# Inverse variance applied to the residual blocks after their last accumulation instead of to the last super-round's activations

## Chip, cores and metric

The kernel runs on one core of one Trainium2 chip. The metric is the device time of one execution in microseconds (us). Before the change three timed runs gave 1086.19, 1089.17 and 1089.94 us; the median is 1089.17 us. The profile that is read below is that of a further execution, which took 1083.84 us. The engines are named as in the profile: PE is TensorE (PEld its weight loads), DVE is VectorE, ACT is ScalarE, POOL is GpSimd and SP is SyncE.

## What is computed

Two layers of a transformer-like trunk on a sequence of 512 positions and width 1024, all in float32. The feed-forward part of a layer is what the change touches:

```python
def _rms(x, gain):
    xf = x.astype(jnp.float32)
    y = xf * lax.rsqrt(jnp.mean(xf * xf, axis=-1, keepdims=True) + EPS)
    return (y * gain.astype(jnp.float32)).astype(x.dtype)
...
    x = x + jnp.concatenate([ya, yb, yc], axis=-1) @ w_out
    u = _rms(x, norm2) @ w_ff1
    return x + jnp.square(jax.nn.relu(u)) @ w_ff2
```

The hidden width is 4096. Since relu followed by a square is homogeneous of degree two, the factor 1/variance of a position can be taken out of it: relu(r h)^2 = r^2 relu(h)^2 with r^2 = 1/(mean(x^2) + EPS).

## The kernel before

Everything is kept transposed, features on the 128 partitions and the 512 positions along the free axis. The residual stream is the tile `xT` (8 k-tiles of 512 positions). Each float32 product is made of three matmuls on high and low parts (`mm3`, L261 to L263). The weights come by DMA as raw tiles of 128x1024 (`raw`, `fraw`; L156 on SP's queue, an accumulating second one at L158 on POOL's queue), ACT rounds them to `whi` (L203), and DVE subtracts to get `wlo` (L204). There are three buffers of each (`HIB` = 3), so weights are prepared up to three jobs ahead of PE. A job is one such weight tile: 24 matmuls of 128x128 by 256 columns.

After two first rounds the feed-forward products use a seven-product scheme in place of eight block products (`ORDER` = A11, S1, S2, A12, S4, S3, A22), which needs sums of raw weight tiles (L214 and L218 on DVE). The hidden width is cut into eight rounds, and two rounds make a super-round (`NS` = 4 of them, s = 0 to 3). `ff1_st(s, rr)` computes the activations of one round in seven jobs, `ff2(s)` adds the second product of a super-round to `xT` in fourteen jobs (dg = 0 and 1 for each of the seven). `ff_pairs` orders them: jobs of `ff2(s)` alternate with jobs of the first product of super-round s + 1, so the activations of s = 3 are made beside `ff2(2)`, and `ff2(3)` runs by itself at the end of the layer. A framework's scheduler fixes the order on each engine; each engine then runs its own list strictly in order.

The scaling is done as follows. The high and low parts that go into the first product are not normalised. On the first visit of a block of `xT` in super-round 0, the block is multiplied by the variance (L1269, `nv` is minus the variance), so that unscaled activations can be added in super-rounds 0 to 2. In super-round 3 the block is multiplied by the inverse variance `r2` on its first visit (L1271), and the activations of that super-round are multiplied by `r2` as well, by `rscale` (L1175), which `act` calls behind the relu (L1179) and the square (L1180) of ACT. `acc` adds or subtracts each finished product to its block (L1272). A block is 2 k-tiles by 256 positions, so each of these DVE instructions works on 128x512 elements. Of a block's last addition `acc` is told by `done_`: in layer 0 `xprep` then makes the high and low parts for the next layer (L328 on DVE), and in layer 1 the block goes out by a DMA on SP's queue (L1274).

Of the kernel before, what the change touches and what calls it, by code (L numbers as in the profile page):

```python
# [16 lines left out]
ALU = mybir.AluOpType  # L17
AX = mybir.AxisListType

P = 128  # L20
# [24 lines left out]
NS = NR // 2  # L45
# [5 lines left out]
def trunk(ctx, tc, x, cols, rows, gate_w, tabs, w_in, w_out, w1, w2, out):  # L51
    nc = tc.nc
    V, A, G, T = nc.vector, nc.scalar, nc.gpsimd, nc.tensor
# [31 lines left out]
    def wt(tag, name):  # L85
        n, bufs = phase["tags"][tag]
        return phase["pool"].tile([P, n], F32, tag=tag, name=nm(name), bufs=bufs)
# [7 lines left out]
    def v3(a, d=HD):  # L95
        return a.rearrange("p (h d) -> p h d", d=d)
# [347 lines left out]
    for l in range(L):  # L444
# [627 lines left out]
        ct, bt = 0, 0  # L1072
# [19 lines left out]
        ct = v3(wt("ct", "ct"), S)  # L1092
# [11 lines left out]
        def bank():  # L1104
            return banks.popleft()

        rr_ = {}
# [24 lines left out]
        def prod1(bk, op, start=True):  # L1132
            bh, bl = xop(op, 0), xop(op, 1)
            prod(bk, lambda kk: bh[:, kk, :], lambda kk: bl[:, kk, :], start)
# [14 lines left out]
        def q2(a):  # L1149
            return v3(a, 256)  # L1150
# [16 lines left out]
        def csplit(s, rr):  # L1167
            u = GU.setdefault((s, rr), {})["c"] = unit_for(s, False)
            A.activation(u[:, 0], q2(ct[:, 0]), AF.Copy)
            V.tensor_tensor(u[:, 1], q2(ct[:, 0]), u[:, 0], ALU.subtract)  # L1170

        def rscale(s, a, n=1):
            if s == NS - 1:
                j = a % 2
                V.tensor_tensor(q2(ct[:, a]), q2(ct[:, a]),  # L1175
                                rr_["r2"][:, j * 256:(j + 1) * 256].unsqueeze(1).broadcast_to((P, 2, 256)), ALU.mult)

        def act(s, a, src, sign):
            A.activation(ct[:, a], src, AF.Relu, scale=sign)  # L1179
            A.activation(ct[:, a], ct[:, a], AF.Square)  # L1180
            rscale(s, a)

        def n1_():
            V.tensor_tensor(ct[:, 4], ct[:, 0], ct[:, 1], ALU.subtract)

        def n2_(s, rr):
            V.scalar_tensor_tensor(ct[:, 5], ct[:, 3], -1.0, ct[:, 4], ALU.mult, ALU.subtract)
            V.tensor_tensor(ct[:, 1], ct[:, 3], ct[:, 1], ALU.subtract)
            gsplit(s, rr, "n", 4)

        def tail_(s, rr):
            gsplit(s, rr, "b", 2)
            V.scalar_tensor_tensor(ct[:, 2], ct[:, 5], -1.0, ct[:, 2], ALU.mult, ALU.subtract)
            gsplit(s, rr, "t", 1)
# [28 lines left out]
        def ff1_st(s, rr):  # L1223
            X = bank()
            prod1(X, 0)
            A.activation(ct[:, 0], X, AF.Copy)
            yield
            Z = bank()
            prod1(Z, 3)
            A.activation(ct[:, 3], Z, AF.Copy)  # L1230
            yield
            prod1(X, 4, False)
            A.activation(ct[:, 1], X, AF.Copy)
            yield
            Y = bank()
            prod1(Y, 1)
            V.tensor_tensor(ct[:, 0], Y, ct[:, 0], ALU.add)
            banks.append(Y)
            act(s, 0, ct[:, 0], 1.0)
            csplit(s, rr)  # L1240
            yield
            prod1(Z, 2, False)
            V.tensor_tensor(ct[:, 1], Z, ct[:, 1], ALU.add)
            banks.append(Z)
            act(s, 1, ct[:, 1], 1.0)
            n1_()
            yield
            prod1(X, 5, False)
            V.tensor_tensor(ct[:, 3], X, ct[:, 3], ALU.add)  # L1249
            act(s, 3, ct[:, 3], -1.0)  # L1250
            n2_(s, rr)
            yield
            prod1(X, 6, False)
            act(s, 2, X, -1.0)
            banks.append(X)
            tail_(s, rr)
            yield

        seen = set()

        def acc(s, dg, i, j, bk, done_=False):
            kx = 4 * i + 2 * dg
            cs_ = slice(j * 256, (j + 1) * 256)
            t_ = xT[:, kx:kx + 2, cs_]
            if s in (0, NS - 1) and (s, dg, i, j) not in seen:
                seen.add((s, dg, i, j))
                b_ = rr_["nv" if s == 0 else "r2"][:, cs_].unsqueeze(1).broadcast_to((P, 2, 256))
                if s == 0:
                    V.scalar_tensor_tensor(t_, t_, -1.0, b_, ALU.mult, ALU.mult)  # L1269
                else:  # L1270
                    V.tensor_tensor(t_, t_, b_, ALU.mult)  # L1271
            V.tensor_tensor(t_, t_, q2(bk), ALU.subtract if i else ALU.add)  # L1272
            if done_ and s == NS - 1 and last:
                nc.sync.dma_start(out[kx * P:(kx + 2) * P, cs_].rearrange("(a p) q -> p a q", p=P), t_)  # L1274

# [6 lines left out]
        def ff2(s):  # L1282
            fin = s == NS - 1 and not last
            X, Z = {}, {}
            for dg in range(2):
                X[dg] = bank()
                prod2(X[dg], s, 0)
                acc(s, dg, 0, 0, X[dg])
                give(s, dg, "c")
                yield  # L1290
            for dg in range(2):
                Z[dg] = bank()
                prod2(Z[dg], s, 3)
                acc(s, dg, 1, 1, Z[dg])
                yield
            for dg in range(2):
                prod2(X[dg], s, 4, False)
                acc(s, dg, 0, 1, X[dg])
                give(s, dg, "n")
                yield  # L1300
# [19 lines left out]
            for dg in range(2):  # L1320
# [7 lines left out]
                yield  # L1328

        gens = {1: (None for r in range(NR) for _ in (ff1_std if r < NSTD else ff1_st)(r // 2, r % 2)),  # L1330
                2: (None for s in range(NS) for _ in ff2(s))}
        bg = None
# [77 lines left out]
```

## Time and profile before

| | value |
|---|---|
| timed runs, median of 3 | 1089.17 us (1086.19 to 1089.94) |
| profiled execution, its own time | 1083.84 us |
| span of its instructions | 1082.1 us |
| PE busy | 1064.9 us, 98% of the span |
| DVE busy | 923.2 us, 85% |
| ACT busy | 624.7 us, 58% |
| POOL busy | 106.2 us, 10% |
| granted clock of TensorE | 0.998 of full speed, that is 2.4 GHz |
| matmuls | 8376 |

Busy times are sums over one profiled execution. Matmuls are pipelined and overlap, so a PE that counts as busy need not run at its peak: what counts is the time from the start of one matmul to the start of the next. Layer 0's feed-forward seven-product part runs from about 270 to 544 us of the span, layer 1's from about 805 to 1078 us.

### The profile page before, as it was taken

What the parts mean: (1) busy time and instruction counts of PE and PEld (TensorE: products, weight loads), DVE (VectorE), ACT (ScalarE), POOL (GpSimd) and SP (SyncE); (2) the same over time, 40 slices, a digit from 0 to 9 for tenths busy, and PEclk for the clock granted to TensorE, in tenths of its full rate; (3) what the DMA queues carried; (4) which work ended last, traced back from release to release, by engine and by line L of the source; (5) the groups of instructions that cost most, each with busy time, mean ns of one, the idle gap of its engine ahead of it and who ended that gap; (6) DMA issues with size and microseconds to landing.
All of it is one profiled execution on the core that took longest, in us unless ns stands there. A gap on an engine that the chain in (4) does not pass through costs nothing.

```text
span 1082.1 us, 20916 instructions
## 1 busy us (share of the span) xinstructions
PE 1064.9 (98%) x8376; PEld 994.8 (92%) x8376; DVE 923.2 (85%) x1566; ACT 624.7 (58%) x1097; POOL 106.2 (10%) x154
## 2 busy tenths in 40 slices
PE   8999999999999999999999999999999999999998
PEld 8999977887999999999999998778789999999998
DVE  7696777899997988999967878688999899799996
ACT  6445655375666666566455466544765666566552
POOL 2030010103010010001002200101000000010100
PEclk9999999999999999999999999999999999999999
DMA  6533121245378486587334221213435866775862
GB/s 215 160 97 98 60 67 50 78 157 127 117 198 230 135 233 180 159 215 192 108 107 162 94 78 60 69 41 136 118 78 157 232 178 179 207 185 168 224 166 99
DMA packets 47346, 151.81 MB, mean 140 GB/s; under 512 B 5632, under 2 KB 8832, under 8 KB 47248
## 3 DMA queue, kind: packets, MB, share of 16 engines
q1 hardware_dynamic: 39184, 121.10, 32.6%
q0 software_dynamic: 8064, 29.36, 15.8%
q8 instruction: 66, 1.08, 0.4%
q14 instruction: 32, 0.26, 0.1%
HBM read 147.86 MB, written 2.13 MB: 139 GB/s over the span
## 4 chain that ended last, share of the span: by engine, by line
PE 72%; DVE 15%; DMA 6%; ACT 4%; issue 2%; SPq 0%; DVEq 0%; ACTq 0%; POOLq 0%
PE at L261 21%; PE at L263 21%; PE at L262 21%; DVE wlo L204 4%; DMA raw<-in_w_dram 4%; DVE rt L719 2%; ACT whi L203 1%; DMA fraw<-in_w_dram 1%; DVE xT L1272 1%; PE at L850 1%; PE at L892 1%; PE at L875 1%; PE at L749 1%; DVE yg L1165 1%; PE at L804 1%
## 5 line engine op out<-in xcount | busy, mean ns | idle before, releaser
L203 ACT ACTIVATE whi<-raw 128x1024 fp32r<-128x1024 f32 (+1 forms) x144 | 150.8, 1047 | 139.5 <-PE at L262 94.4
L204 DVE TENSOR_TENSOR wlo<-raw,whi 128x1024 fp32r<-128x1024 f32 (+1 forms) x144 | 174.1, 1209 | 39.9 <-ACT whi L203 39.5
L203 ACT ACTIVATE whi<-fraw 128x1024 fp32r<-128x1024 f32 x122 | 129.1, 1059 | 93.2 <-PE at L262 74.3
L261 PE MATMUL at<-yg,whi 128*128 128x256 f32 (+1 forms) x592 | 180.5, 308 | 0.0
L263 PE MATMUL at<-yg,wlo 128*128 128x256 f32 (+1 forms) x592 | 179.2, 303 | 0.5 <-DVE wlo L204 0.5
L262 PE MATMUL at<-xhl,whi 128*128 128x256 f32 (+1 forms) x576 | 178.4, 310 | 0.0
L262 PE MATMUL at<-yg,whi 128*128 128x256 f32 (+1 forms) x560 | 170.0, 304 | 0.0
L261 PE MATMUL at<-whi,xhl 128*128 128x256 f32 (+1 forms) x576 | 165.0, 286 | 2.0 <-ACT whi L203 2.0
L262 PE MATMUL at<-wlo,xhl 128*128 128x256 f32 (+1 forms) x576 | 161.6, 280 | 0.3 <-DVE wlo L204 0.3
L263 PE MATMUL at<-whi,xhl 128*128 128x256 f32 (+1 forms) x576 | 161.5, 280 | 0.0
L261 PE MATMUL at<-xhl,whi 128*128 128x256 f32 (+1 forms) x512 | 161.4, 315 | 0.0
L263 PE MATMUL at<-xhl,wlo 128*128 128x256 f32 (+1 forms) x512 | 160.7, 314 | 0.0
L204 DVE TENSOR_TENSOR wlo<-fraw,whi 128x1024 fp32r<-128x1024 f32 x122 | 148.6, 1218 | 7.3 <-ACT whi L203 6.5
L263 PEld LDWEIGHTS at<-yg,wlo 128*128 128x128 f32 x592 | 111.1, 188 | 6.2 <-DVE wlo L204 0.9
L261 PEld LDWEIGHTS at<-yg,whi 128*128 128x128 f32 x592 | 111.3, 188 | 5.7 <-issue 1.7
L262 PEld LDWEIGHTS at<-xhl,whi 128*128 128x128 f32 x576 | 108.5, 188 | 7.6 <-issue 0.5
L261 PEld LDWEIGHTS at<-whi,xhl 128*128 128x128 f32 x576 | 109.2, 190 | 3.2 <-ACT whi L203 2.1
L262 PEld LDWEIGHTS at<-wlo,xhl 128*128 128x128 f32 x576 | 109.1, 189 | 0.5 <-DVE wlo L204 0.5
L262 PEld LDWEIGHTS at<-yg,whi 128*128 128x128 f32 x560 | 105.6, 189 | 4.2 <-DVE yg L1003 0.5
L263 PE MATMUL at<-xbx,wlo 128*128 128x256 f32 x384 | 106.8, 278 | 2.7 <-DVE wlo L204 2.6
L263 PEld LDWEIGHTS at<-whi,xhl 128*128 128x128 f32 x576 | 109.0, 189 | 0.2
L261 PE MATMUL at<-xbx,whi 128*128 128x256 f32 x384 | 106.5, 277 | 0.2 <-DVE ct L1249 0.2
(287 smaller groups left out, 2440.0 us busy)
## 6 DMA issues: line engine op xcount, KB each, us to landing
fraw<-in_w_dram SPq DMA_DIRECT2D x90, 512.0 KB, 4.6
raw<-in_w_dram SPq DMA_DIRECT2D x66, 512.0 KB, 4.5
raw<-in_w_in_dram SPq DMA_DIRECT2D x34, 512.0 KB, 3.3
fraw<-in_w_dram POOLq DMA_DIRECT2D x34, 512.0 KB, 6.1
raw<-in_w_dram POOLq DMA_DIRECT2D x22, 512.0 KB, 7.5
raw<-in_w_out_dram SPq DMA_DIRECT2D x16, 512.0 KB, 3.2
rowb<-drow SPq DMA_DIRECT2D x16, 256.0 KB, 3.7
raw<-in_w_in_dram SPq DMA_DIRECT2D x12, 256.0 KB, 4.7
```

The lines of the kernel that those rows point to most:

```text
L203: A.activation(hi[:, cs_], raw[:, cs_], AF.Copy)
L204: V.tensor_tensor(lo[:, cs_], raw[:, cs_], hi[:, cs_], ALU.subtract)
L261: T.matmul(o, sh, mh, start=first, stop=False, skip_group_check=skip)
L262: T.matmul(o, sh, ml, start=False, stop=False, skip_group_check=skip)
L263: T.matmul(o, sl, mh, start=False, stop=last, skip_group_check=skip)
L719: V.tensor_tensor(r10[:, oo:oo + n, a:a + 32], z10[:, oo:oo + n, b:b + 32], tb(S_, n, a, a + 32), ALU.mult)
L749: T.matmul(sc[r][:, g * 256:g * 256 + nk], qTA[g][r * 64:(r + 1) * 64, c * P:(c + 1) * P], kTA[r * 64:(r + 1) * 64, k0:k0 + nk], start=Tru ...
L804: T.matmul(po[r * 64:(r + 1) * 64, g * P:(g + 1) * P], vt[:w, r * 64:(r + 1) * 64], p1[:w, u * P:(u + 1) * P], start=g == 0, stop=p2 is No ...
L850: T.matmul(sp[:, :nk], qTB[rs, pr, n * P:(n + 1) * P], kTB[rs, pr, :nk], start=True, stop=False)
L875: T.transpose(pt[:, b * P:(b + 1) * P], scs[r][:, b * P:(b + 1) * P], ident)
L892: T.matmul(pobs[pr][r * 64:(r + 1) * 64, n * P:(n + 1) * P], zbv[b][:, h * 64:(h + 1) * 64], ps[r][:, b * P:(b + 1) * P], start=b == 0, st ...
L1165: V.tensor_tensor(lo, c4(a, a + 2), hi, ALU.subtract)
```

## The change

The activations of the last super-round are no longer scaled, and a block is multiplied by `r2` not on its first visit in that super-round but behind its last addition.

```diff
-        def rscale(s, a, n=1):
-            if s == NS - 1:
-                j = a % 2
-                V.tensor_tensor(q2(ct[:, a]), q2(ct[:, a]),
-                                rr_["r2"][:, j * 256:(j + 1) * 256].unsqueeze(1).broadcast_to((P, 2, 256)), ALU.mult)
-
-        def act(s, a, src, sign):
+        def act(a, src, sign):
             A.activation(ct[:, a], src, AF.Relu, scale=sign)
             A.activation(ct[:, a], ct[:, a], AF.Square)
-            rscale(s, a)
...
-            if s in (0, NS - 1) and (s, dg, i, j) not in seen:
-                seen.add((s, dg, i, j))
-                b_ = rr_["nv" if s == 0 else "r2"][:, cs_].unsqueeze(1).broadcast_to((P, 2, 256))
-                if s == 0:
-                    V.scalar_tensor_tensor(t_, t_, -1.0, b_, ALU.mult, ALU.mult)
-                else:
-                    V.tensor_tensor(t_, t_, b_, ALU.mult)
+            bc_ = lambda n: rr_[n][:, cs_].unsqueeze(1).broadcast_to((P, 2, 256))
+            if s == 0 and (dg, i, j) not in seen:
+                seen.add((dg, i, j))
+                V.scalar_tensor_tensor(t_, t_, -1.0, bc_("nv"), ALU.mult, ALU.mult)
             V.tensor_tensor(t_, t_, q2(bk), ALU.subtract if i else ALU.add)
+            if done_ and s == NS - 1:
+                V.tensor_tensor(t_, t_, bc_("r2"), ALU.mult)
             if done_ and s == NS - 1 and last:
                 nc.sync.dma_start(out[kx * P:(kx + 2) * P, cs_].rearrange("(a p) q -> p a q", p=P), t_)
```

In the changed kernel the addition stands at L1262 and the new multiply at L1264; L1177, L1180, L1181, L1186 and L1242 are what L1184, L1187, L1188, L1193 and L1249 were. The lists of SP and of POOL are the same row for row. On DVE rows go and move. This is the middle of the last round of activations in layer 0, before the change, where a wait of PE will be read; `ct` holds the activations, `at` are PSUM banks, `r` is `r2`:

```order
708 L1175 TENSOR_TENSOR ct_2847<-ct_2847,r_3134 128x512
709 L1272 TENSOR_TENSOR xT<-xT,at_2946 128x2x256
710 L1184 TENSOR_TENSOR ct_2847<-ct_2847 128x512
711 L204 TENSOR_TENSOR wlo_5862<-fraw_2848,whi_5861 128x1024
712 L1271 TENSOR_TENSOR xT<-xT,r_3134 128x2x256
713 L1249 TENSOR_TENSOR ct_2847<-at_2948,ct_2847 128x512
714 L204 TENSOR_TENSOR wlo_5900<-raw_74,whi_5899 128x1024
715 L1175 TENSOR_TENSOR ct_2847<-ct_2847,r_3134 128x512
716 L214 TENSOR_TENSOR raw_74<-raw_73,raw_74 128x1024
717 L1187 SCALAR_TENSOR_TENSOR ct_2847<-ct_2847 128x512
```

And the same place of DVE's list in the changed kernel:

```order
698 L1177 TENSOR_TENSOR ct_2847<-ct_2847 128x512
699 L1262 TENSOR_TENSOR xT<-xT,at_2946 128x2x256
700 L204 TENSOR_TENSOR wlo_5856<-fraw_2848,whi_5855 128x1024
701 L1242 TENSOR_TENSOR ct_2847<-at_2948,ct_2847 128x512
702 L204 TENSOR_TENSOR wlo_5893<-raw_74,whi_5892 128x1024
703 L1180 SCALAR_TENSOR_TENSOR ct_2847<-ct_2847 128x512
704 L1181 TENSOR_TENSOR ct_2847<-ct_2847 128x512
705 L1262 TENSOR_TENSOR xT<-xT,at_2944 128x2x256
```

Three multiplies (708, 712, 715) are gone from this stretch, and the sum of raw weights (716) has moved behind the work on the activations.

At the close of layer 0, where `ff2(3)` runs alone, this stood on DVE before (L328 makes the next layer's low parts):

```order
747 L1272 TENSOR_TENSOR xT<-xT,at_2950 128x2x256
748 L204 TENSOR_TENSOR wlo_6263<-raw_73,whi_6262 128x1024
749 L328 SCALAR_TENSOR_TENSOR xhl<-xT,pcol,xhl 128x512 x2
750 L1272 TENSOR_TENSOR xT<-xT,at_2943 128x2x256
751 L204 TENSOR_TENSOR wlo_6297<-fraw_2848,whi_6296 128x1024
752 L328 SCALAR_TENSOR_TENSOR xhl<-xT,pcol,xhl 128x512 x2
```

In the changed kernel the same place of DVE's list reads:

```order
734 L1262 TENSOR_TENSOR xT<-xT,at_2950 128x2x256
735 L1264 TENSOR_TENSOR xT<-xT,r_3134 128x2x256
736 L204 TENSOR_TENSOR wlo_6252<-raw_73,whi_6251 128x1024
737 L328 SCALAR_TENSOR_TENSOR xhl<-xT,pcol,xhl 128x512 x2
738 L1262 TENSOR_TENSOR xT<-xT,at_2943 128x2x256
739 L204 TENSOR_TENSOR wlo_6287<-fraw_2848,whi_6286 128x1024
740 L1264 TENSOR_TENSOR xT<-xT,r_3134 128x2x256
```

A multiply now stands between the addition and the parts for the next layer, eight times in this stretch.

The last rows of DVE in the whole program were additions alone:

```order
1491 L1272 TENSOR_TENSOR xT<-xT,at_9188 128x2x256
1492 L204 TENSOR_TENSOR wlo_12542<-raw_75,whi_12541 128x1024
1493 L1272 TENSOR_TENSOR xT<-xT,at_9186 128x2x256
1494 L1272 TENSOR_TENSOR xT<-xT,at_9188 128x2x256
1495 L1272 TENSOR_TENSOR xT<-xT,at_9186 128x2x256
```

In the changed kernel they are these:

```order
1476 L1262 TENSOR_TENSOR xT<-xT,at_9178 128x2x256
1477 L1264 TENSOR_TENSOR xT<-xT,r_9365 128x2x256
1478 L1262 TENSOR_TENSOR xT<-xT,at_9180 128x2x256
1479 L1264 TENSOR_TENSOR xT<-xT,r_9365 128x2x256
1480 L1262 TENSOR_TENSOR xT<-xT,at_9178 128x2x256
1481 L1264 TENSOR_TENSOR xT<-xT,r_9365 128x2x256
```

Behind the very last addition there is now one multiply before the output DMA can go.

## Rows read from the trace of the kernel before

**Rows 1.** The page's head and its part 1: busy us, share of span, instructions.
```profile
span 1082.1 us, 20916 instructions
PE 1064.9 (98%) x8376; PEld 994.8 (92%) x8376; DVE 923.2 (85%) x1566; ACT 624.7 (58%) x1097; POOL 106.2 (10%) x154
```

**Rows 2.** Windows: stretch, length, busy us of PE, PEld, DVE, ACT, POOL; clock, DMA.
```profile
440.00:480.00 40.00, 40.00 (x355) 40.00 (x354) 38.20 (x44) 24.37 (x29) 3.49 (x4) 1.00 0.67 184
480.00:520.00 40.00, 38.04 (x324) 37.06 (x323) 38.76 (x47) 23.05 (x27) 3.45 (x4) 1.00 0.78 199
520.00:544.00 24.00, 24.00 (x206) 24.00 (x205) 21.29 (x25) 12.80 (x15) 0.00 (x0) 1.00 0.26 89
860.00:920.00 60.00, 60.00 (x532) 60.00 (x531) 52.94 (x58) 38.39 (x47) 4.34 (x5) 1.00 0.66 188
```

**Rows 3.** Instructions by source line: L1175, L1271 and L1272, ns min/median/max.
```profile
L1175 DVE TENSOR_TENSOR ct<-ct,r x16: 682/692/696, 449.3 to 1040.9; 128x512 f32<-128x512 f32 x16
L1271 DVE TENSOR_TENSOR xT<-xT,r x16: 680/683/693, 474.0 to 1061.2; 128x512 f32<-128x512 f32 x16
L1272 DVE TENSOR_TENSOR xT<-xT,at x112: 673/680/689, 279.1 to 1078.0; 128x512 f32<-128x512 f32 x112
```

**Rows 4.** Timeline of PE, layer 0: start us, us, what, [idle before it, releaser].
```profile
433.67 0.28 PE L261 MATMUL at<-xbx,whi 128*128 128x256 f32 x1
...
498.51 0.28 PE L263 MATMUL at<-gx,wlo 128*128 128x256 f32 x1
498.96 0.36 PE L261 MATMUL at<-xbx,whi 128*128 128x256 f32 x1 [0.17 <-DVE ct L1249]
...
506.15 0.39 PE L263 MATMUL at<-gx,wlo 128*128 128x256 f32 x1 [1.06 <-DVE wlo L204]
...
519.05 0.28 PE L261 MATMUL at<-yg,whi 128*128 128x256 f32 x1
...
543.90 0.28 PE L261 MATMUL at<-whi,xhl 128*128 128x256 f32 x1
```

**Rows 5.** Timeline of DVE in the last round of activations, layer 0.
```profile
497.52 0.68 DVE L1271 TENSOR_TENSOR xT<-xT,r 128x512 f32<-128x512 f32 x1
498.13 0.68 DVE L1249 TENSOR_TENSOR ct<-at,ct 128x512 f32<-128x512 f32 x1
...
500.18 0.69 DVE L1175 TENSOR_TENSOR ct<-ct,r 128x512 f32<-128x512 f32 x1 [0.23 <-ACT ct L1180]
...
504.88 1.22 DVE L204 TENSOR_TENSOR wlo<-fraw,whi 128x1024 fp32r<-128x1024 f32 x1
506.01 0.68 DVE L1175 TENSOR_TENSOR ct<-ct,r 128x512 f32<-128x512 f32 x1
```

**Rows 6.** Timeline of PE, layer 1, from the last wait ahead of the changed stretch.
```profile
942.52 0.28 PE L261 MATMUL at<-gx,whi 128*128 128x256 f32 x1
...
1052.52 0.28 PE L262 MATMUL at<-yg,whi 128*128 128x256 f32 x1
...
1053.92 0.28 PE L261 MATMUL at<-yg,whi 128*128 128x256 f32 x1
...
1077.73 0.28 PE L263 MATMUL at<-gx,wlo 128*128 128x256 f32 x1
```

**Rows 7.** Timeline of DVE at the close of layer 0.
```profile
537.06 1.22 DVE L204 TENSOR_TENSOR wlo<-raw,whi 128x1024 fp32r<-128x1024 f32 x1
...
546.68 1.41 DVE L328 SCALAR_TENSOR_TENSOR xhl<-xT,pcol,xhl 128x512 fp32r<-128x512 f32 x2
```

**Rows 8.** Timeline of PE: first matmuls of the last job of layer 0, and layer 1's third k-tile.
```profile
541.07 0.28 PE L261 MATMUL at<-yg,whi 128*128 128x256 f32 x1
...
552.38 0.28 PE L261 MATMUL at<-whi,xhl 128*128 128x256 f32 x1
```

**Rows 9.** Timeline of all engines behind the last matmul.
```profile
1078.05 0.69 DVE L1272 TENSOR_TENSOR xT<-xT,at 128x512 f32<-128x512 f32 x1 [2.03 <-PE at L263]
1078.76 0.37 SPq L1274 DMA_DIRECT2D out_dram<-xT  x1
```

More of the change, by code (lines that the diff above doesn't have):

```diff
@@ L1238, in ff1_st @@
             banks.append(Y)
-            act(s, 0, ct[:, 0], 1.0)
+            act(0, ct[:, 0], 1.0)
             csplit(s, rr)
@@ L1244, in ff1_st @@
             banks.append(Z)
-            act(s, 1, ct[:, 1], 1.0)
+            act(1, ct[:, 1], 1.0)
             n1_()
@@ L1249, in ff1_st @@
             V.tensor_tensor(ct[:, 3], X, ct[:, 3], ALU.add)
-            act(s, 3, ct[:, 3], -1.0)
+            act(3, ct[:, 3], -1.0)
             n2_(s, rr)
@@ L1253, in ff1_st @@
             prod1(X, 6, False)
-            act(s, 2, X, -1.0)
+            act(2, X, -1.0)
             banks.append(X)
```

## Prediction

> **What bounds the kernel now.** The page's head comes first: PE counts as busy for 1064.9 of 1082.1 us, DVE for 923.2 [rows 1]. Such a PE can lose time in two ways: by waits, and by a longer time from one matmul to the next. So I read the windows, which give the number of matmuls in a stretch, and then the timeline of PE around the changed lines.
>
> In a quiet stretch of layer 1 PE starts 532 matmuls in 60 us, 112.8 ns each, and never waits, although DVE is busy for 52.94 of the 60 us, 88% [rows 2]. In the two rounds of layer 0 in which the last super-round's activations are made, DVE is fuller: 38.20 of 40 us from 440 to 480 and 38.76 of 40 us from 480 to 520, 96% together, and in the second of them PE starts 324 matmuls where the first has 355 [rows 2]. So here DVE is what PE waits for. The timeline of PE shows where: 0.17 us for the subtraction at L1249, which frees a PSUM bank, at 498.96, then 1.06 us for a `wlo` at 506.15, then some small waits up to 519.05 [rows 4]. On DVE the subtraction of 498.13 stands right behind a multiply of L1271, which does not need to be there yet, and ahead of the `wlo` of 504.88 stands a multiply of L1175, which waited 0.23 us for ACT [rows 5].
>
> What these waits cost in all: from 433.67 to 498.51 there are 572 steps from matmul to matmul in 64.84 us, 113.4 ns each. From 498.51 to 519.05 there are 150 steps in 20.54 us; at 113.4 ns they would take 17.0 us, so 3.5 us are lost. From 519.05 to 543.90 there are 211 steps in 24.85 us, 117.8 ns each and not 113.4, without any wait; at 113.4 ns they would take 23.9 us, so another 0.9 us is lost [rows 4]. PE has two paces in this trace, at the same granted clock of 1.00 [rows 2], and holds one until its next wait. Layer 1 shows the same: 934 steps from 942.52 to 1052.52 in 110.00 us are 117.8 ns each, then come 4 steps in 1.40 us, then 210 steps to 1077.73 in 23.81 us, 113.4 ns each [rows 6]. What chooses the pace behind a wait the trace does not tell.
>
> **The change, part by part.** *Removed from DVE's full stretch.* The 16 multiplies of L1175 (8 per layer) go. The 16 of L1271 (8 per layer) leave their place; 7 of each 8 stand before 520 us in layer 0, from 474.0 us on. Each has a duration of 0.68 to 0.69 us [rows 3], but the next instruction starts 0.61 us after it (497.52 to 498.13) [rows 5], so I take 0.60 us. In layer 0 that is (8 + 7) x 0.60 = 9.0 us out of 77.0 us of DVE work in 80 us; 68.0 us remain, 85%. That is less than the 88% at which PE did not wait at all [rows 2]. So I take the waits between 498.51 and 519.05 as gone. From below: nothing, if they come from the order or from transfers and not from the amount of DVE work; from above: all 3.5 us. I take the 3.5, since the three multiplies that stand in front of the instructions waited for are exactly among those that go. If no wait is left, PE has no reason to leave its pace of 113.4 ns, and the 0.9 us up to 543.90 go too. Together 4.4 us, of which some 0.3 may be matmuls that the trace lost (933 steps are in it, 39 jobs of 24 are 936).
>
> In layer 1 PE ran slower when DVE was full, so it waited less: the 4 steps of 1.40 us would have taken 0.47 at 117.8 ns, so 0.93 us are lost. But behind that wait PE took the fast pace. Without the wait it keeps 117.8 ns for the last 210 steps, which costs 210 x 4.4 ns = 0.93 us [rows 6]. I take 0 for layer 1; bounds: 0.93 gained, if it changes pace anyway, and 0.93 lost, if the wait stays and the fast pace is not found again.
>
> *A rule that speaks against this.* Over the whole span DVE is busy for 85%, PE's weight loads for 92%; from 480 to 520 us it is the other way round, 38.76 us of DVE against 37.06 us of weight loads [rows 1, 2]. The Trainium skill, page "Perfetto Trace Analysis", section "Identifying the Most-Contended Engine", says to optimise the engine of the highest occupancy first, and to judge TensorE by the busy share of its weight loads and not of its matmuls. Read over the span, that makes the relief of DVE worth nothing: the 4.4 us drop out, the 0.65 us of the program's end (below) stay, and the time is 1089.8 us. Read over the 40 us it names DVE, and the 4.4 us stay in the sum. I go by the stretch, since that is where PE waits.
>
> *Moved to the close of layer 0.* From 520 to 544 us DVE is busy for 21.29 of 24 us [rows 2], and seven more multiplies, 4.2 us, come in: 25.5 us, 1.5 more than there are. Each stands between an addition and the next `wlo`, or ahead of the next layer's parts (L328); behind it queue both, and PE waits for `wlo`. I cost it at nothing, and this is the cover: the `wlo` of the last job is done at 537.06 + 1.22 = 538.28, PE starts that job at 541.07, 2.8 us later [rows 7, 8], and DVE now comes to 520 us without a backlog. The last parts of L328 are done at 546.68 + 1.41 = 548.09, and the first matmul that reads k-tile 6 starts at 552.38, 4.3 us later [rows 7, 8]. If the cover is gone, the most that it costs is 7 x 0.60 = 4.2 us.
>
> *Moved to the end of the program.* Behind the last addition (1078.05) nothing covers the multiply; the output DMA was issued at 1078.76 [rows 9] and now waits for one more instruction, whose price is between 0.60 (spacing) and 0.69 us (duration) [rows 3, 5]. I take 0.65. The other seven multiplies of layer 1 stand where DVE waits for PE: the last addition had 2.03 us of idle time before it [rows 9]. The lists of SP and POOL are unchanged; their DMAs only follow a DVE that frees buffers sooner.
>
> **The sum.** -4.4 (layer 0) + 0 (layer 1) + 0.65 (end) = -3.75 us. Against the profiled execution's own 1083.84 us that is 1080.1 us, 0.35% less. The median of the timed runs, 1089.17, is 5.3 us above the profiled execution; long stretches at the slow pace could make such differences between executions (the 532 steps of the quiet 60 us at 117.8 in place of 112.8 ns would be 2.7 us [rows 2]), and most of them lie ahead of the change. So I take the difference from the median: 1089.17 - 3.75 = 1085.4 us. A difference of 0.3%, 3.3 us, is about what a measurement of this kernel can tell from no change, so the forecast lies just beyond it.
>
> **The rivals.**
> *Layer 1 is in luck too.* If PE comes out of its wait near 942 at the fast pace, the 934 steps cost 4.1 us less and the last 210 stay fast, 0.93 us: 1085.4 - 5.1 = 1080.3 us. Before, such luck would have been eaten by DVE's backlog, as in layer 0; now it can last. For it: of the two rounds that I read, one began fast and one slow [rows 4, 6]. Against it: the wait itself stands ahead of the change.
>
> *DVE's work is not what the time hangs on.* If the waits stay, because ACT or a raw tile is late and not because DVE is full, only the end counts: 1089.17 + 0.65 = 1089.8 us. This is also what the rule above gives when it is read over the span. For it: DVE itself waits there (0.23 us for ACT) [rows 5]. Against it: the waits end with DVE instructions [rows 4], and 9.0 us of work in front of them go.
>
> *The pace is lost.* If PE enters the stretch of layer 0 at the slow pace, the 933 steps to 543.90 cost 933 x 4.4 ns = 4.1 us and eat the 4.4: 1089.17 - 0.3 + 0.65 = 1089.5 us. For it: it is PE's pace in layer 1 [rows 6]. Against it: at 433.67 it took the fast one [rows 4], and the change comes later.
>
> *The other side: the multiplies stop PE at the close of layer 0.* DVE has 1.5 us too much to do from 520 to 544. From the point where it is more than 2.8 us late at the `wlo` of the last jobs, PE waits, and all 4.2 us of multiplies can come to lie on its path: 1085.4 + 4.2 = 1089.6 us, and with the slow pace for the 72 steps that layer 1 makes up to 552.38 [rows 4, 8], 0.3 us, 1089.9; a little slower than before. It is more than 0.3% slower only where such a wait leaves PE at the slow pace for several hundred steps more. For it: 25.5 us of work in 24. Against it: the backlog that DVE brought into this stretch is gone.
>
> **How the numbers follow.** The forecast 0.44 (0.34 of it beyond 0.3%, since it lies so near), layer 1 in luck 0.12, DVE not the cause 0.13, pace lost 0.18, the multiplies stop PE 0.13 (0.11 counted as slower, for a longer slow pace). Faster by over 0.3%: 0.34 + 0.12 = 0.46; slower: 0.11; the same: 0.10 + 0.13 + 0.18 + 0.02 = 0.43. The likeliest is 1085.4; its own range is 1083.5 to 1087.5. The range of 8 in 10 reaches to the luck of layer 1 and to the other side: 1080.0 to 1090.3.
>
> **What would show it.** In the changed profile: no waits of PE on `wlo` or L1242 between 498 and 519; matmuls of layer 0 from about 434 to 540 at 113.4 ns throughout; DVE near 85% from 440 to 520; one multiply (0.65 us) between the last addition and the output DMA. The prediction is wrong if PE waits for `wlo` between 530 and 545 (multiplies in the way), if the same waits stand at 498 to 519 with a DVE that is now less full (transfers or ACT), or if the waits are gone and the matmuls of either layer nevertheless stand at 117.8 ns.

## The result, and the profile after

The changed kernel took 1078.01 us (median of 14 executions, 1075.52 to 1086.79) against 1085.85 us for the kernel before on the same chip (14 executions, 1080.27 to 1096.47): a ratio of 0.9932, 95% interval 0.9907 to 0.9958, so it is faster, by twice what was forecast, and the time lies below the range. Its profiled execution took 1081.89 us. The same kernel was compared four more times, on two chips (below): 0.9986 (0.9957 to 1.0015), 0.9986 (0.996 to 1.0013), 0.995 (0.9914 to 0.9986) and 0.995 (0.9917 to 0.9983). A ratio leaves out executions in a slow state and is not simply the quotient of the two medians beside it, here and below.

The page's head and its part 1, after, which answer to [rows 1]:

```profile
span 1080.1 us, 20906 instructions
PE 1063.0 (98%) x8376; PEld 993.1 (92%) x8376; DVE 913.4 (85%) x1550; ACT 625.2 (58%) x1097; POOL 107.3 (10%) x154
```

DVE has 16 instructions and 9.8 us less. The profiled span fell by only 2.0 us, so one must look by stretch. The windows of after (columns as in [rows 2]):

```profile
440.00:480.00 40.00, 40.00 (x355) 40.00 (x354) 36.96 (x40) 24.88 (x30) 3.48 (x4) 1.00 0.73 193
480.00:520.00 40.00, 40.00 (x355) 40.00 (x354) 34.80 (x38) 24.50 (x28) 3.45 (x4) 1.00 0.79 201
520.00:544.00 24.00, 24.00 (x211) 23.87 (x211) 23.90 (x34) 13.62 (x18) 0.53 (x1) 1.00 0.27 84
965.00:1075.00 110.00, 110.00 (x934) 110.00 (x934) 95.38 (x104) 58.00 (x67) 7.80 (x9) 1.00 0.63 169
```

From 480 to 520 us PE now has 355 matmuls, not 324 [rows 2], and is never idle (a window also counts those that began just ahead of it). From 965 to 1075, in layer 1, it is never idle either, but slower: the 932 steps from 965.18 to 1074.95 take 109.77 us, 117.8 ns each. PE's timeline of after shows both:

```profile
426.76 0.28 PE L263 MATMUL at<-yg,wlo 128*128 128x256 f32 x1
...
537.26 0.28 PE L263 MATMUL at<-gx,wlo 128*128 128x256 f32 x1
537.50 0.36 PE L261 MATMUL at<-yg,whi 128*128 128x256 f32 x1
...
540.32 0.28 PE L261 MATMUL at<-whi,xhl 128*128 128x256 f32 x1
...
548.80 0.28 PE L261 MATMUL at<-whi,xhl 128*128 128x256 f32 x1
...
957.05 0.28 PE L262 MATMUL at<-yg,whi 128*128 128x256 f32 x1
...
964.96 0.38 PE L263 MATMUL at<-xbx,wlo 128*128 128x256 f32 x1 [0.16 <-DVE wlo L204]
965.18 0.28 PE L261 MATMUL at<-xbx,whi 128*128 128x256 f32 x1
...
1074.95 0.28 PE L263 MATMUL at<-gx,wlo 128*128 128x256 f32 x1
```

From here on I count alike in all traces: the last 1000 steps from matmul to matmul of a layer, which in layer 0 end with the first matmul that reads `xhl` for layer 1 (540.32 here), and in layer 1 with the program's last matmul. After: 540.32 - 426.76 = 113.56 us in layer 0 and 1074.95 - 957.05 = 117.90 us in layer 1. Before: 118.20 us (up to the 543.90 of [rows 4]) and 117.79 us (up to the 1077.73 of [rows 6]). So layer 0 gained 4.64 us, layer 1 lost 0.11.

The one new gap of PE is 0.24 us before the 537.50 and 0.20 us behind it, where a step is 0.113: 0.20 us lost. DVE's timeline of after shows what is late there:

```profile
536.07 0.68 DVE L1264 TENSOR_TENSOR xT<-xT,r 128x512 f32<-128x512 f32 x1
536.68 0.68 DVE L1262 TENSOR_TENSOR xT<-xT,at 128x512 f32<-128x512 f32 x1
...
545.43 1.41 DVE L328 SCALAR_TENSOR_TENSOR xhl<-xT,pcol,xhl 128x512 fp32r<-128x512 f32 x2 [0.70 <-ACT xhl L327]
```

The addition at L1262 reads the PSUM bank that the last job writes into; it ends at 536.68 + 0.68 = 537.36, behind a multiply of the change, and PE starts at 537.50. The parts of L328 are done at 546.84, 1.96 us before the matmul of 548.80 that needs them (before: 4.3 us). Behind the last matmul all engines of after, where [rows 9] has no multiply:

```profile
1075.27 0.69 DVE L1262 TENSOR_TENSOR xT<-xT,at 128x512 f32<-128x512 f32 x1 [1.41 <-PE at L263]
1075.99 0.69 DVE L1264 TENSOR_TENSOR xT<-xT,r 128x512 f32<-128x512 f32 x1
1076.71 0.37 SPq L1266 DMA_DIRECT2D out_dram<-xT  x1
```

From the start of the addition to the issue of the DMA it is 1.44 us instead of 0.71: 0.73 us more. Layer 0, layer 1 and the end make -4.64 + 0.11 + 0.73 = -3.8 us. The span shows 2.0, mainly because the 1249 steps ahead of the last 1000, in which no line changed, took 142.53 and 143.80 us where they took 141.55 and 142.78 before. So the profiled pair agrees with the forecast's sum, and the 14 timed executions don't. What is to be explained is why layer 1 stood still, and whether 0.9932 is the rule.

### The profile page after: what moved, and what is told of

It reads as the page before. It is cut to its first block, busy times and chain, and to the rows that moved or that the text cites. A ratio compares the mean times of both kernels' runs of the same rounds, so it can differ in the third digit from the quotient of the medians.

```text
span 1080.1 us, 20906 instructions
## 1 busy us (share of the span) xinstructions
PE 1063.0 (98%) x8376; PEld 993.1 (92%) x8376; DVE 913.4 (85%) x1550; ACT 625.2 (58%) x1097; POOL 107.3 (10%) x154
## 3 DMA queue, kind: packets, MB, share of 16 engines
HBM read 147.86 MB, written 2.13 MB: 139 GB/s over the span
## 4 chain that ended last, share of the span: by engine, by line
PE 76%; DVE 11%; DMA 7%; ACT 4%; issue 2%; SPq 0%; DVEq 0%; POOLq 0%; ACTq 0%
PE at L261 23%; PE at L263 22%; PE at L262 22%; DMA raw<-in_w_dram 5%; DVE wlo L204 3%; DVE rt L719 2%; DMA fraw<-in_w_dram 1%; ACT whi L203 1%; PE at L850 1%; PE at L892 1%; PE at L875 1%; PE at L749 1%; DVE yg L1165 1%; PE at L804 1%; PE at L973 1%
```

## The experiments

The first four separate the two halves of the change. Each expectation names the theories that it weighs; those of the last four carry the theory that was left.

**e1: the multiplies of the activations dropped, nothing moved.**

```diff
             A.activation(ct[:, a], ct[:, a], AF.Square)
-            rscale(s, a)
```

> The kernel before without the multiply of the last super-round's activations (L1175), the multiply of the blocks left on the first visit; the factor on these activations is left out of the computation. DVE work from 440 to 520 us of layer 0 falls from 77.0 by 8 x 0.60 = 4.8 to 72.2 of 80 us (90%). Theory 1 (PE waits because DVE is full there): the waits of PE shrink to under a quarter of 3.5 us, nothing is added at the end, ratio to before near that of the whole change, 0.993 to 0.995. Theory 2 (the multiplies matter because they stand in the chain from ACT's square to the parts of the activations): all of the gain, 0.992 to 0.993, since the chain is freed entirely. Theory 3 (only the multiplies of the blocks in front of the PSUM reader matter): 0.998 to 1.000.

**e2: the block's multiply moved, those of the activations kept.** `acc` as in the change, `act` as before.

> The kernel before with the multiply of the blocks moved behind the last addition, the multiply of the activations left in; the last super-round is scaled twice. DVE work from 440 to 520 us of layer 0 falls by 7 x 0.60 = 4.2 to 72.8 of 80 us (91%). Theory 1 (DVE full): most of the waits go, ratio 0.994 to 0.997 (0.65 us more at the end). Theory 2 (chain from ACT's square): nothing won, 0.65 us lost, 1.000 to 1.001. Theory 3 (multiplies of the blocks): all of the gain, 0.993.

**e3: both gone** (and e8, the same kernel on another chip).

```diff
             V.tensor_tensor(t_, t_, q2(bk), ALU.subtract if i else ALU.add)
-            if done_ and s == NS - 1:
-                V.tensor_tensor(t_, t_, bc_("r2"), ALU.mult)
```

> The changed kernel without the multiply behind the last addition; the blocks are left unscaled. If the eight multiplies per layer at the close cost only the one behind the program's last addition: 0.65 us less than the changed kernel, ratio 0.9926 beside its 0.9932, and the time from the last matmul's start to the span's end 0.6 to 0.7 us shorter. If they stop PE at the close of layer 0: 3 to 4 us less, 0.990.

> The changed kernel without the multiply behind the last addition, once more; the blocks are left unscaled. It gave 0.9966 where the changed kernel had given 0.9932, though it does less. Theory A (scatter of the pace): it comes out at or just below the other runs of the changed kernel in this call, 0.65 us less. If leaving the multiply out really costs time: above them again.

**e4: the change, and DVE's work put back beside the chain.** In the last super-round `act` has one more multiply, whose result nobody reads.

```diff
             A.activation(ct[:, a], ct[:, a], AF.Square)
+            if side:
+                V.tensor_tensor(rr_["lnv"], ct[:, a], rr_["r2"], ALU.mult)
```

> The changed kernel with a multiply of the activations by the inverse variance put back at the place of L1175 on DVE, but into a tile that nobody reads, so that nothing but DVE's own list waits for it. Theory 1 (DVE full): DVE work from 440 to 520 us of layer 0 rises by 4.8 us to 72.8 of 80 (91%) and some of the gain is given back, as in the move alone: ratio 0.994 to 0.997. Theory 2 (chain from ACT's square to the parts): the chain stays free, the gain stays, 0.993. Both: the time at the end as in the changed kernel.

Times (medians of 12 executions each): e1 1083.65 us, ratio 0.9978 (0.9946 to 1.001); e2 1084.69, 0.9992 (0.9964 to 1.0019); e3 1082.36, 0.9966 (0.9938 to 0.9994); e4 1084.34, 0.9988 (0.9966 to 1.001), all beside the same before of 1084.83. e8: 1086.64, 0.9965 (0.9931 to 0.9998), beside 1087.35. The ratios that the theories gave started from the 0.9932 of the first comparison, and in none of e1 to e4 was one of them met. e8 lies below the changed kernel on the same chip (0.9986, below), so nothing shows that leaving the last multiply out costs time. The intervals overlap: the times alone don't tell the halves apart. The waits of PE do. In e1, e3 and e8 the view of waits is empty from 450 to 560 us and from 985 us to the end. In e2 it has, for those two stretches:

```profile
PE at L263 <- DVE wlo L204: 1.1, 2, 0.8
PE at L261 <- ACT whi L203: 0.4, 1, 0.4
...
PE at L261 <- ACT whi L203: 0.3, 1, 0.3
PE at L263 <- DVE wlo L204: 0.3, 1, 0.3
```

and in e4:

```profile
PE at L263 <- DVE wlo L204: 0.3, 1, 0.3
...
PE at L261 <- ACT whi L203: 0.4, 1, 0.4
PE at L263 <- DVE wlo L204: 0.3, 1, 0.3
```

A layer at the slow pace has few waits in the old code too (0.3 us in before's layer 1), and layer 0 of e1, e8 and e4 is such a layer (117.8 ns). So the layers at the fast pace count: layer 1 of e1 and of e8 and both of e3 have no wait, both of e2 have some, and so has layer 1 of e4. The 16 multiplies on the activations make the waits: without them there is none, even with the block's multiply in its old place (e1), and moving that one alone leaves 1.5 and 0.6 us (e2), where before has 1.9 in layer 0. The same multiplies beside the chain of the activations, on the same engine and behind the same squares, still make 0.7 us in the fast layer and 0.3 in the slow one (e4): part of it is the place that they take in DVE's list, and not only that ACT and DVE go on from their results. How large each part is, two traces don't settle.

What makes the time differ more than that is the pace. e3's windows of 40 us in layers 0 and 1:

```profile
480.00:520.00 40.00, 40.00 (x356) 40.00 (x355) 35.65 (x40) 24.00 (x28) 3.45 (x4) 1.00 0.72 198
...
1005.00:1045.00 40.00, 40.00 (x355) 40.00 (x354) 34.45 (x38) 24.24 (x28) 3.49 (x4) 1.00 0.77 199
```

Here PE has the fast pace from end to end of both feed-forwards, and the execution took 1073.31 us; e8, the same kernel, has 117.8 ns through the whole of layer 0 and took 1086.36 us. Neither has a wait in the changed stretches.

**e5 to e7: the changed kernel twice more, and the kernel before as its own control**, with e8 on a second chip.

> The changed kernel once more, word for word. Theory A (the last 1000 steps of each layer take 118 us before, whatever PE's pace, and 113.4 or 117.8 us after, by the pace that PE happens to hold; a gain of 4.6 us in a layer at the fast pace, none at the slow): the runs scatter by up to 9 us, the ratio lies between 0.992 and 0.998, and the profile has per layer 113.3 to 114 us (fast) or 117.8 to 118 (slow). Theory B (the change wins 7.4 us in every execution, the profiled pair was an exception): ratio 0.993 again, both layers short.

> The kernel before once more, as a control. Ratio 1.000, its interval says how far draws alone move a ratio. Theory A: the last 1000 steps of each layer take 116.5 to 118.5 us, with about 3.5 us of waits where the pace is fast and about 1 us where it is slow. Theory B says nothing of it.

> The changed kernel a third time, for the scatter of its ratio and one more profile. Theory A: 0.992 to 0.998, and again one of the two lengths in each layer. Theory B: 0.993, both layers short.

e5: 1088.16 us, 0.9986; e7: 1086.58 us, 0.9986; the control e6: 1087.21 us, 1.0004 (0.9974 to 1.0034). The gain of the first comparison did not come back: theory B's 0.993 lies outside both intervals, and theory A's 0.992 to 0.998 is missed too, by less than the intervals. (e6's layer 1, 118.67 us, is a little above the 118.5 expected of it, with a late tile ahead of the stretch.) The profiles show how an execution can gain nothing: in e5's layer 0 and e7's layer 1 PE is at the slow pace and never idle. e7's timeline of PE, layer 1:

```profile
961.24 0.28 PE L262 MATMUL at<-yg,whi 128*128 128x256 f32 x1
...
1079.02 0.28 PE L263 MATMUL at<-gx,wlo 128*128 128x256 f32 x1
```

1000 steps in 117.78 us, without one wait. e5's layer 1 is fast but took 117.37 us: a tile of weights came late, 12.11 us in the chain, and PE stood for `wlo` (the chain and the timeline of PE, then the window behind it):

```profile
957.28 12.11 DMA raw<-in_w_dram
```

```profile
974.16 0.39 PE L263 MATMUL at<-xbx,wlo 128*128 128x256 f32 x1 [2.13 <-DVE wlo L204]
```

```profile
975.40:978.30 2.90, 2.90 (x15) 2.90 (x15) 2.90 (x4) 0.23 (x2) 0.24 (x1) 0.50 0.90 263
```

That wait costs twice: soon behind it the granted clock is 0.50 for 2.90 us, the 1.2 GHz level, with 15 matmuls where some 25 fit at full clock.

**e9 and e10: the change in one layer only.** In e9 the new code runs where `not last`, in e10 where `last`; the other layer is as before. e10's edit in `acc`, for example:

```diff
-            if s in (0, NS - 1) and (s, dg, i, j) not in seen:
+            if (s == 0 or s == NS - 1 and not last) and (s, dg, i, j) not in seen:
...
+            if done_ and s == NS - 1 and last:
+                V.tensor_tensor(t_, t_, rr_["r2"][:, cs_].unsqueeze(1).broadcast_to((P, 2, 256)), ALU.mult)
```

> The change in layer 0 alone; layer 1 as before, so the end has no multiply of the change behind its last addition. Theory A (PE has two paces, 113.4 and 117.8 ns a matmul, and takes one anew at each wait; before, the last 1000 steps of a layer take 117 to 119 us at either pace, since DVE holds PE up where PE is fast; with the change they take 113.4 us when PE is fast and 117.8 when it is slow, without a wait on DVE): layer 0's last 1000 steps at 113.4 or 117.8 us with under 0.5 us of waits on DVE, layer 1's at 117 to 119 us; ratio between 0.996 and 1.000. The prediction's own sum: layer 0 always 4.4 us shorter, ratio 0.996. If layer 0 still shows 2 us of waits on DVE, both fall.

> The change in layer 1 alone; layer 0 as before. Theory A: layer 0's last 1000 steps 117 to 119 us with waits on DVE where PE is fast, layer 1's 113.4 or 117.8 us without; 0.74 us of multiply at the end; ratio between 0.997 and 1.001. The prediction's sum: layer 1 gains nothing and the end costs 0.65 us, ratio 1.0006, and the last 1000 steps of layer 1 stay near 117.8 us.

e9: 1080.78 us, 0.9961 (0.9932 to 0.999); e10: 1080.45 us, 0.9956 (0.9931 to 0.998), beside a before of 1084.17. By the prediction's sum e10 should have been at 1.0006: its interval leaves that out. It is also below theory A's 0.997 to 1.001, by less than the interval. The two halves add up to 0.83%, where the whole change gave 0.50% twice on the same chip (below); the intervals are too wide to make anything of that. The waits in e9's layer 1 (as before):

```profile
PE at L263 <- DVE wlo L204: 1.0, 2, 0.8
PE at L261 <- ACT whi L203: 0.4, 1, 0.4
```

and in e10's layer 0 (as before):

```profile
PE at L263 <- DVE wlo L204: 1.4, 2, 1.1
PE at L261 <- ACT whi L203: 0.4, 1, 0.4
```

The changed layer of each has none, and both were fast: 113.64 us for the last 1000 steps in e9's layer 0, 113.33 in e10's layer 1, of which this is the timeline of PE:

```profile
961.22 0.28 PE L262 MATMUL at<-yg,whi 128*128 128x256 f32 x1
...
1074.55 0.28 PE L263 MATMUL at<-gx,wlo 128*128 128x256 f32 x1
```

The waits follow the code, layer by layer, within one execution.

**e11 and e12: the changed kernel again, on the third chip, that of e9 and e10.**

> The changed kernel, word for word, once more. Theory A: each layer's last 1000 steps at 113.4 or 117.8 us, drawn anew, so a gain between 0 and 8.5 us over an execution of before, 4 on the mean; ratio 0.994 to 0.999, and at 0.9966 or so over all the runs of it. Rival: the first comparison's 0.9932 is the rule, and the two at 0.9986 belong to the chip that they ran on; then 0.993 here.

> As the run before it, for a second profile and a second ratio on the same chip: theory A 0.994 to 0.999, rival 0.993. If the two ratios of this call differ by more than 0.003, the scatter of a single comparison is that large.

1081.21 and 1081.57 us, 0.995 both, as theory A expected. The rival's 0.993 lies inside both intervals, so these two runs don't exclude it for this chip. On each chip the two ratios agree (0.9986 twice, then 0.995 twice): that the share of slow draws differs from chip to chip is not ruled out. e11 is the trace in which both layers are fast:

```profile
427.20 0.28 PE L263 MATMUL at<-yg,wlo 128*128 128x256 f32 x1
...
540.77 0.28 PE L261 MATMUL at<-whi,xhl 128*128 128x256 f32 x1
...
955.42 0.28 PE L262 MATMUL at<-yg,whi 128*128 128x256 f32 x1
...
1068.81 0.28 PE L263 MATMUL at<-gx,wlo 128*128 128x256 f32 x1
```

113.57 and 113.39 us, and its span is 1074.0 us. e12's layer 0 took the slow pace behind a wait of 0.82 us at 436.28, another late tile, ahead of the changed code:

```profile
436.28 0.39 PE L263 MATMUL at<-xbx,wlo 128*128 128x256 f32 x1 [0.82 <-DVE wlo L204]
```

The wait is at the same job of the layer as e5's, where the chain leads from the late raw tile over a sum of raw tiles (L214) to `wlo`. PE stands there in after too (0.16 us at 964.96, and the slow pace of its layer 1 begins behind it), and has a step over 135 ns there, 932 to 934 steps from the layer's end, in ten of the 28 feed-forwards, old and changed. So one thing that sets a layer's pace for the changed stretch lies ahead of it, in code that the change does not touch.

All profiles of the two schemes, the last 1000 steps of a layer in us:

| scheme, trace | layer 0 | layer 1 |
|---|---|---|
| as before: before | 118.20 | 117.79 |
| as before: e6 | 117.25 | 118.67 |
| as before: e10's layer 0, e9's layer 1 | 117.26 | 116.87 |
| changed: after | 113.56 | 117.90 |
| changed: e5 | 117.78 | 117.37 (late tile) |
| changed: e7 | 113.63 | 117.78 |
| changed: e11 | 113.57 | 113.39 |
| changed: e12 | 118.58 (late tile) | 113.33 |
| changed: e9's layer 0, e10's layer 1 | 113.64 | 113.33 |

The six old layers lie between 116.87 and 118.67: five came into the changed stretch at the fast pace and have the waits, and one, before's layer 1, came in slow. Of the twelve new ones seven lie between 113.33 and 113.64 and five between 117.37 and 118.58. The means are 117.67 and 115.32: 2.35 us per layer, 4.7 for two, less 0.73 at the end: 4.0 us, an estimate from so few layers.

## Why the prediction was wrong

**DVE's backlog is what PE waits for, and the change takes it away: right.** In all twelve changed layers the view of waits is empty from 450 to 560 us and from 985 us to the end (the 0.20 us at 537.50 are too short for it); five of the six old ones have 1.4 to 2.0 us there, and the sixth, before's layer 1 at the slow pace, 0.3. Eight of the twelve were fast, and these show it; four were slow. The share of DVE was priced too low, 85%: it is 36.96 + 34.80 = 71.76 of 80 us, 90%, 5.2 us less than before and not 9.0, since the windows hold 13 instructions fewer, not 15, and more of the other work. It was enough all the same. The rule weighed in the prediction (the Trainium skill, page "Perfetto Trace Analysis", section "Identifying the Most-Contended Engine"), read over the whole span, would have made this relief worth nothing; e9 and e10 disagree, at 0.9961 and 0.9956. The prediction went by the stretch instead, and there it was right.

**Layer 0, 4.4 us: right in mechanism and size where PE comes in fast** (118.20 to 113.56 in the profiled pair). Two of its readings need a correction that changes little. The quiet pace is 113.3 ns and not 112.8, which divides 60 us by a count that takes in matmuls begun ahead of the window. And no matmul was lost between 433.67 and 543.90: 433.67 is the fourth matmul of its job, so 39 jobs make 933 steps, and all traces hold 8376 matmuls; the 0.3 us that might have come off the 4.4 fall away.

**Layer 1, "I take 0 for layer 1": the step that failed.** It took the pace of one profiled execution, 117.8 ns, for layer 1's own. The runs show a pace that changes from execution to execution, a draw as it were: layer 1 took 113.33 to 113.39 us in e10, e11 and e12, 117.78 and 117.90 in e7 and after. In the old code the draw hardly mattered, because a fast PE ran into DVE's backlog. Before's layer 0 shows it in one window: 38.76 us of DVE for 324 matmuls [rows 2] would be 42.5 us for the 355 that a fast PE makes in 40 us, an estimate with the same work per matmul. So the old last 1000 steps took 117 to 119 us whichever pace was drawn (slow in one old layer only). That the waits of a fast layer cost about what the slow pace costs, 1000 x 4.4 ns, is chance. The change lets a fast layer keep its 4.4 us, in both layers alike (e9, e10), and gives a slow one nothing (117.79 us before, 117.78 and 117.90 in e7 and after). That is the rival "Layer 1 is in luck too", which the prediction had at 1080.3 us with 0.12, and the rival "The pace is lost" for layer 0 (e5, e12): not two exceptions but the two faces of the change. The mean over the draws, -4.0 us, is close to the predicted -3.75, but by luck, for it has other terms: 2.35 + 2.35 - 0.73 in place of 4.4 + 0 - 0.65.

**The base, "the median, 1089.17": 4 us too high.** It came from three executions. In the comparison itself the kernel before took 1085.85 us: of the 7.4 us between the forecast 1085.4 and the measured 1078.01, the base makes 3.3 and the size of the change 4.1 (-7.84 in place of -3.75). Over 131 executions of before in all comparisons (e6 among them) the median is 1085.3 us, over 62 of the changed kernel 1083.0, and the means are 1085.9 and 1082.5: -3.4 us, 0.31%. These mix chips; the means of the first comparison and of the second and third chip differ by -7.8, -0.7 and -4.3 us. The single comparisons give -0.68, -0.14, -0.14, -0.50 and -0.50%. So the first one stands at the lucky end, and its time of 1078.01 lies between a profiled execution with both layers fast (e11, 1075.66 us) and one with one slow layer (e12, 1081.16 us). That its executions drew the fast pace more often is argued from this, not shown: timed executions leave no trace.

**Close of layer 0, cost at nothing: wrong by 0.20 us, and at another place.** Not `wlo` is late but the addition that frees the last job's PSUM bank. All four changed layers 0 that came in fast lose 0.19 to 0.21 us in waits; e3, without the multiplies, loses none (113.34 us). The layers 0 at the slow pace (e5, e12) have no gap there. The cover at k-tile 6 held (1.96 us left).

**End, 0.65 us: measured 0.73** in the profiled pair; in every trace with the multiply the span ends 5.13 to 5.16 us behind the start of the last matmul, in those without it 4.40 to 4.42.

**Open:** what chooses the pace behind a gap, and why the share of slow draws seems to differ from comparison to comparison, by the chip or otherwise.

## What to carry to other kernels

Where one execution shows an engine at a pace that it keeps without a reason in the code, treat that pace as a draw: ask what the change is worth under each pace, and give the forecast as a mean of those, not as the one trace. A backlog on another engine can hide the better draw, and so removing it pays only where the draw is good; a comparison of some ten executions then moves by as much as the gain. Take the base from as many executions as there are, and read a gain of some 0.3% from the traces' stretches before the medians.

## What the hardware showed

PE runs the same stream of 256-column matmuls, at a granted clock of 1.00, at 113.3 or 117.8 ns, and changes between them only at a gap. In the 28 feed-forwards of the 14 traces no stretch of 15 matmuls or more between two gaps (steps over 135 ns) changes pace inside, up to the 2250 of e8's layer 0 (slow) and of e3's (fast). Of 54 gaps between such stretches, 31 led from fast to fast, 17 from fast to slow, 6 from slow to fast, and none from slow to slow. Over the 2250 steps of one layer the two paces are 10 us apart (2250 x 4.4 ns), 0.9% of the kernel. Behind the gap of 2.13 us in e5 the granted clock was 0.50 for about 3 us; behind those of 0.82 us in e12 and 1.60 us in e2 it stayed at 1.00. The length alone does not decide it: at the head of layer 0's seven-product part PE stands for 1.98 to 2.00 us in 13 traces (2.34 in e4), and soon after it starts again the clock falls to the 1.2 GHz level for some 16 steps in six of the 14 traces, which costs 1.6 us each time (16 steps of 0.213 in place of 0.113 us), and stays at 2.4 GHz in the other eight. The same stretch in before and in e12:

```profile
282.40:285.90 3.50, 3.50 (x33) 3.50 (x33) 3.50 (x4) 1.55 (x2) 0.87 (x1) 1.00 0.77 268
...
282.40:285.90 3.50, 3.50 (x19) 3.50 (x18) 3.01 (x4) 0.26 (x1) 0.87 (x1) 0.52 0.74 268
```
